# A hybrid diffusion backbone on one core: long-convolution filters 256 channels at a time, interleaved with the gates of layer 0

## The chip, the core and the metric

The kernel runs on one core of one Trainium2 chip. A core has a matrix engine (TensorE, "PE" in the profile, with its weight loads shown as "PEld"), a vector engine (VectorE, "DVE"), an activation engine (ScalarE, "ACT"), a general engine (GpSimd, "POOL"), and a sync engine ("SP") that issues this kernel's DMAs. On-chip data lie in SBUF; matmuls write to PSUM, which has eight banks of 512 fp32 columns. The metric is the time of one execution in device microseconds.

## The reference, cut to what matters

Four trunk layers run over 512 latent and 256 context tokens of width 1024. Layers 0 and 3 are multi-head latent attention, layer 1 is windowed attention, layer 2 is a Hyena long convolution. Two parts of it are touched by the change.

The gate of an attention layer is a projection of the normalised, modulated input `h`; the attention's output is multiplied by its SiLU:

```
cq_x, ckv_x, kr_x, gate_x = jnp.split(hx @ w_in, split_at, axis=-1)
...
y_x = (o_x.reshape(b, n, A_WIDTH) * jax.nn.silu(gate_x)) @ w_out
```

The filters of layer 2 depend on weights alone, so they can be made at any time before layer 2. A small network gives 64 features for each tap; a product with `f_w3` gives the taps, a decay is multiplied on, and layer 2 needs the transform of the taps (2 orders, 2 directions, 1024 channels, once for 512 and once for 256 taps):

```
h = jnp.sin(freq * (z @ f_w1 + f_b1))
h = jnp.sin(freq * (h @ f_w2 + f_b2))
h = (h @ f_w3).astype(jnp.float32).reshape(n, 2, C_ORDER, C_WIDTH)
...
return h * jnp.exp(-t[:, :, None, None] * deltas)
```

## The kernel before, in words

**Numbers.** fp32 values are split in a high part (rounded to a shorter float by ScalarE) and a low part (the rest, by VectorE or GpSimd), and each product is three matmuls: high x high, high x low, low x high.

**Memory.** Two arenas in SBUF are managed by hand: `R` for split operands (118 KB in each partition and a further 24 KB, the "swing") and `F` for fp32 (54 KB). `rl` and `fl` take long-lived blocks from the bottom; `rs` and `fs` take staging slots (8 KB and 4 KB) from the top. `turns_r` and `turns_f` say among how many free slots the one that was freed longest ago is chosen. In PSUM there are four single banks (`a()`, in turn) and two pairs of banks (`s()`, in turn; `halves()` are the four banks of the two pairs).

**Streams of weights.** `W` is the queue of all weights in the order of their use. `take` hands out the next one; `pump` goes ahead: it issues DMAs into fp32 slots (at most `cap_d` staged) and makes high and low parts (at most `cap_w` held). `M` is the same for the modulation weights `w_mod`, which aren't split. A mod unit is 2 MB of `w_mod` in four pieces (`mod_chunk`, L434), 16 matmuls and, for shift and scale, four transposes. The four units of layer 0 must be done before its input can be modulated; later units are "fillers", spread over the layers.

**Order.** The program states an order, and a scheduler that simulates the engines turns it into one fixed order for each engine: an instruction that it expects to be ready may pass an earlier one that it expects to wait. On the chip every engine keeps to its fixed order.

**The start** (`run`, L1668 to L1683) is one loop of steps. `filters` is a generator: before its first `yield` lie the small network, the first `f_w3` weights, the transform table and the decays. Then come 24 steps and 3 for the last spectrum. There are eight groups (c, o, e): 512 channels, order, even or odd part. In `taps` (L1356) each of six tap tiles has two matmuls (L1369), a product with the decay on VectorE (L1371), a high part on ScalarE (L1375) and a low part on GpSimd (one of six on VectorE, L1377). `spectrum` (L1388) of the group before has 30 matmuls (L1397) into PSUM pairs, a ScalarE copy (L1401), two VectorE operations (L1402, L1403), and DMAs to `kd` in DRAM (L1407). The loop puts the four mod units of layer 0 at steps 4, 8, 12 and 16, and the six `pre` (L530: norm, transposes, modulation and split of a token tile of `h`) at every second step from 16 on. At steps 25, 27 and 29 the first weights of layer 0 are pumped.

**Layer 0** (`layer_A`, L691): keys for six tiles (L734, 320 columns), queries for six tiles (L762, 512 columns), six filler units among them; each tile is normalised (`normed`, L701) and transposed. Then come the gates (L769): eight groups of 128 channels, each 48 matmuls (`mm_ch`, L588) into single banks, half of them of 512 columns and half of 256, then `gate2` (L344: tanh on ScalarE, one VectorE operation). Then `rotary`, values, projections, the attention, and `w_out_phase` (L592), in which the next layer's `pre` run. Layer 3 uses the same code for 512 query tokens. In `layer_A` the low parts of weights are made by VectorE (`lo_pool` False); during the start they are made by GpSimd.

Of the kernel before, what the change touches and what calls it, by code (L numbers as in the profile page):

```python
# [19 lines left out]
P = 128  # L20
D = 1024
KD = 8
# [8 lines left out]
WX = {25: (3, 2), 27: (3, 2), 29: (3, 3)}  # L31
# [10 lines left out]
MI = (4, 8, 12, 16)  # L42
PS = 16
PD = 2
WP = 2

R_WORDS = 118 * 256
F_WORDS = 54 * 256 - 64
# [222 lines left out]
class Kern:  # L271
    def __init__(self, ctx, tc, io):
# [16 lines left out]
        self.fillers, self.mg = [], {}  # L289

# [301 lines left out]
    def w_out_phase(self, L, og, wkey, order, last, hook):  # L592
# [11 lines left out]
        for n, t in enumerate(order):  # L604
# [43 lines left out]
        if nxt is not None:  # L648
            self.W.pump(self.W.cap_w + 1, self.W.cap_w)
        for b in g:  # L650
            b.free()
# [20 lines left out]
    def want_A(self, L, j, ctx_out):  # L672
        io = self.io
        w = io["a_w_in"][j].rearrange("(k p) n -> p k n", p=P)
        for k in range(0, KD, 2):
# [3 lines left out]
        for c in range(8):  # L679
            self.W.want(("gate", c), w[:, :, 832 + P * c:960 + P * c])  # L680
# [10 lines left out]
    def layer_A(self, L, j, h, ctx_out, last):  # L691
# [5 lines left out]
        og = self.fl(KD * T)  # L697
# [69 lines left out]

        spans = [(0, NX), (NX, NC)] if ctx_out else [(0, NX)]
        for c in range(8):  # L769
# [480 lines left out]
    def filters(self, j):  # L1250

        nc, io = self.nc, self.io
        self.kd = self.dram.tile([2, 8, P, 1536], F32, name="kd")
        fp = self.fl(4 + 128 + 64)
        fv = fp.ap
        w1, w2 = fv[:, 4:68], fv[:, 68:132]
        zt = self.fl(T)
# [13 lines left out]
        sdr = Ring(self, "rl", 2 * 6 * 512, 2)  # L1271
        w3r = Ring(self, "rs", 2 * 2 * 512, 2)
# [3 lines left out]
        biasr = Ring(self, "fl", 512, 1)  # L1276

        def load_w3(c, o):

            st = self.fs(1024)  # L1280
            sv = st.v(2, 512)
            for d in range(2):
                c0 = d * 2048 + o * 1024 + 512 * c
                for half in range(2):
                    nc.sync.dma_start(out=sv[64 * half:64 * half + 64, d], in_=w3[:, c0:c0 + 512])
            sd = self.fs(1024)
            sdv = sd.v(2, 512)
            nc.gpsimd.tensor_tensor(sdv[:, 0], sv[:, 0], sv[:, 1], op=ALU.add)
            nc.gpsimd.tensor_tensor(sdv[:, 1], sv[:, 0], sv[:, 1], op=ALU.subtract)
            wv = w3r.next().v(2, 2, 512)  # L1290
            nc.scalar.activation(wv[:, 0], sdv, AF.Copy)
            nc.vector.tensor_tensor(wv[:, 1], sdv, wv[:, 0].bitcast(F32), op=ALU.subtract)
            st.free()
            sd.free()
            wvs[c, o] = wv
            biases[c, o] = bias = biasr.next()
            nc.sync.dma_start(out=bias.ap[0:1], in_=io["c_filt_bias"][j, o:o + 1, 512 * c:512 * c + 512])

        def load_ft(i):
            for c0, n in ((0, 1024), (1024, 256)):  # L1300
                st = self.fs(n)
                nc.sync.dma_start(out=st.ap, in_=io["ftab"][:, i, c0:c0 + n])
                nc.scalar.activation(ftv[:, i, 0, c0:c0 + n], st.ap, AF.Copy)
                nc.gpsimd.tensor_tensor(ftv[:, i, 1, c0:c0 + n], st.ap, ftv[:, i, 0, c0:c0 + n].bitcast(F32), op=ALU.subtract)
                st.free()

        two_pi = 2 * math.pi
# [490 lines left out]
```

## Time and profile before

| | us |
|---|---|
| median of 3 runs | 1953.55 (1951.68 to 1954.86) |
| profiled execution | 1953.32 |
| its span in the trace | 1951.5 |
| TensorE busy in the span | 1820.0 (93%) |
| VectorE busy | 1182.5 (61%) |
| first matmul of the filters | 23.4 |
| first key matmul of layer 0 | 150.6 |
| first and last gate matmul of layer 0 | 239.7, 313.2 |

How to read the rows: a group's row has the line, the engine, the operation, the tile written and those read, the shape, the count, then busy time, mean ns of one, and the idle time of the engine just before them with what ended it. In the timeline and in the chain of waits a row starts with its start and duration in us; brackets hold the idle time ahead of it and its releaser. A row of the table of stretches has the stretch, its length, busy time (and instructions) of PE, PEld, DVE, ACT and POOL, the granted clock, the share of time that the DMA engines were busy and GB/s. Matmuls are pipelined, so a matmul's duration is longer than the distance to the next one's start. DMA rows give count, KB each and us from issue to landing.

### The profile page before, as it was taken

To read this page: it belongs to the slowest core of one execution; us is meant where nothing else is said; L and a number is where in the kernel's file an instruction comes from. 1 tells how busy PE (TensorE), PEld (TensorE's weight loads), DVE (VectorE), ACT (ScalarE), POOL (GpSimd) and SP (SyncE) were. 2 spreads that over 40 slices of the span, in tenths; PEclk is the share of its full clock that TensorE was granted. 3 is DMA by queue.
4 is the path that set the end of the run, shared out by engine and by line. 5 is a ranking of instruction groups with operands and counts; after the bars stand their busy time and mean duration, and the time that the engine had idled before them with its cause. 6 is when DMAs were issued, how large, how long until landed. Compare 5 with 4: busy or idle time off the path is not lost.

```text
span 1951.5 us, 30304 instructions
## 1 busy us (share of the span) xinstructions
PE 1820.0 (93%) x11628; PEld 1576.6 (81%) x11628; DVE 1182.5 (61%) x2364; ACT 812.3 (42%) x1686; POOL 521.6 (27%) x523
## 2 busy tenths in 40 slices
PE   5879799999999899999989899999998998999998
PEld 3557588999988888888868699999987777889986
DVE  6684134787755367676675445566668553477663
ACT  3473132555544255565664422222222343354451
POOL 5561000000213321221231344444445221000120
PEclk9999899999999999999999999999999999999999
DMA  7857521001133112222362622222221335310121
GB/s 214 259 175 226 158 78 31 22 24 43 44 109 117 57 48 83 76 67 67 99 223 103 204 60 85 70 74 76 76 77 60 122 120 154 87 33 23 44 76 54
DMA packets 186356, 186.31 MB, mean 95 GB/s; under 512 B 16600, under 2 KB 164952, under 8 KB 186212
## 3 DMA queue, kind: packets, MB, share of 16 engines
q1 hardware_dynamic: 186212, 184.39, 30.6%
q8 instruction: 91, 1.49, 0.3%
q14 instruction: 53, 0.43, 0.1%
HBM read 160.24 MB, written 24.12 MB: 94 GB/s over the span
## 4 chain that ended last, share of the span: by engine, by line
PE 77%; DVE 10%; DMA 6%; ACT 3%; issue 3%; POOL 1%; SPq 0%; POOLq 0%; DVEq 0%; ACTq 0%
PE pb L588 13%; PE pb L622 11%; PE pa L588 10%; PE pb L873 5%; PE pa L912 4%; PE pa L1068 3%; PE pa L1049 3%; DMA arena_f<-in_w_mod_dram 3%; PE pa L1525 2%; PE pa L1558 2%; PE pa L442 2%; PE pa L898 2%; PE pa L1177 2%; PE pb L577 2%; PE pb L578 2%
## 5 line engine op out<-in xcount | busy, mean ns | idle before, releaser
L588 PE MATMUL pb<-arena_r 128*128 128x512 f32 (+1 forms) x1536 | 293.2, 345 | 8.1 <-DVE arena_f L1498 3.6
L588 PEld LDWEIGHTS pb<-arena_r 128*128 128x128 f32 x1536 | 239.3, 192 | 40.7 <-issue 3.8
L341 ACT ACTIVATE arena_r<-pa 128x384 fp32r<-128x384 f32 (+2 forms) x382 | 175.3, 478 | 198.5 <-PE pa L898 68.2
L342 DVE TENSOR_TENSOR arena_r<-pa,arena_r 128x384 fp32r<-128x384 f32 (+2 forms) x382 | 199.7, 537 | 86.6 <-ACT arena_r L341 84.9
L588 PE MATMUL pa<-arena_r,swing_R 128*128 128x512 f32 (+1 forms) x816 | 165.9, 355 | 0.6 <-DVE arena_r L342 0.4
L588 PEld LDWEIGHTS pa<-arena_r,swing_R 128*128 128x128 f32 x816 | 132.2, 188 | 21.8 <-DVE arena_r L342 0.6
L873 PE MATMUL pb<-arena_r 128*128 128x384 f32 (+1 forms) x720 | 141.4, 337 | 3.0 <-ACT arena_r L341 1.8
L233 POOL TENSOR_TENSOR swing_R<-arena_f,swing_R 128x1024 fp32r<-128x1024 f32 (+1 forms) x33 | 77.1, 2340 | 200.5 <-ACT swing_R L230 150.7
L873 PEld LDWEIGHTS pb<-arena_r 128*128 128x128 f32 x720 | 119.0, 188 | 5.1 <-ACT arena_r L341 2.5
L668 POOL TENSOR_TENSOR arena_f<-arena_f 128x128 f32<-128x128 f32 (+1 forms) x44 | 20.9, 474 | 364.1 <-DVE small L881 180.1
L622 PE MATMUL pb<-arena_r 128*128 128x512 f32 x480 | 115.2, 393 | 0.0
L358 POOL TENSOR_SCALAR small<-small 128x1 f32<-128x1 f32 x68 | 17.8, 262 | 349.1 <-ACT trash L564 135.6
L622 PEld LDWEIGHTS pb<-arena_r 128*128 128x128 f32 x480 | 89.5, 188 | 20.0 <-issue 1.1
L233 POOL TENSOR_TENSOR arena_r<-swing_F,arena_r 128x1024 fp32r<-128x1024 f32 x34 | 84.6, 2492 | 76.0 <-ACT arena_r L230 73.9
L912 PE MATMUL pa<-arena_r 128*128 128x256 f32 x624 | 91.4, 286 | 2.1 <-DVE arena_r L342 2.1
L912 PEld LDWEIGHTS pa<-arena_r 128*128 128x128 f32 x624 | 81.7, 190 | 4.8 <-ACT arena_r L341 2.5
L1068 PE MATMUL pa<-swing_R,arena_r 128*128 128x256 f32 x576 | 80.2, 289 | 5.1 <-DVE arena_f L348 3.8
L877 DVE TENSOR_REDUCE small<-pb 128x1 f32<-128x768 f32 (+1 forms) x80 | 67.5, 846 | 21.6 <-PE pb L873 20.7
L880 ACT ACTIVATE arena_f<-pb,small 128x768 f32<-128x768 f32 (+1 forms) x80 | 65.2, 816 | 32.9 <-DVE small L878 26.5
L1068 PEld LDWEIGHTS pa<-swing_R,arena_r 128*128 128x128 f32 x576 | 72.9, 192 | 7.3 <-DVE arena_f L348 5.2
L442 PE MATMUL pa<-arena_f,cst 128*32 128x256 f32 x744 | 57.0, 407 | 23.3 <-DMA arena_f<-in_w_mod_dram 23.0
L230 ACT ACTIVATE arena_r<-swing_F 128x1024 fp32r<-128x1024 f32 x34 | 36.2, 1063 | 101.5 <-PE pb L588 93.7
(266 smaller groups left out, 4239.6 us busy)
## 6 DMA issues: line engine op xcount, KB each, us to landing
arena_f<-in_w_mod_dram SPq DMA_DIRECT2D x93, 512.0 KB, 4.8
swing_F<-in_c_w_in_dram SPq DMA_DIRECT2D x31, 512.0 KB, 4.1
kd<-arena_f SPq DMA_DIRECT2D x48, 256.0 KB, 3.4
arena_f<-in_a_w_in_dram SPq DMA_DIRECT2D x24, 512.0 KB, 4.2
arena_f<-kd SPq DMA_DIRECT2D x16, 768.0 KB, 4.5
arena_f<-in_b_w_in_dram SPq DMA_DIRECT2D x20, 512.0 KB, 4.2
x<-arena_f SPq DMA_DIRECT2D x18, 512.0 KB, 4.1
arena_f<-in_a_w_out_dram SPq DMA_DIRECT2D x16, 512.0 KB
```

The source lines that it names most:

```text
L233: eng.tensor_tensor(lo, view, hi.bitcast(F32), op=ALU.subtract)
L341: self.nc.scalar.activation(hi, src, AF.Copy)
L342: self.nc.vector.tensor_tensor(lo, src, hi.bitcast(F32), op=ALU.subtract)
L442: nc.tensor.matmul(ps[32 * j:32 * j + 32, n0:n0 + 256], self.cst[:, 4 * kh + j, :], w[:, j, :], start=(kh == 0), stop=(kh == 1), skip_grou ...
L588: nc.tensor.matmul(out, l, rhs(part, k, i), start=(k == 0 and q == 0), stop=(k == kt - 1 and q == 2))
L622: nc.tensor.matmul(ys[:, 512 * hf:512 * hf + 512], ov[:, part, k], wt[:, 0, 512 * hf:512 * hf + 512], start=(k == 0 and q == 0), stop=(k = ...
L873: nc.tensor.matmul(S[:, 512 * b:512 * b + w], l, r[:, k0 + w * b:k0 + w * b + w], start=(q == 0), stop=(q == 4))
L877: nc.vector.tensor_reduce(mx, Sv, axis=AX.XY, op=ALU.max)
L880: nc.scalar.activation(pr.v(nb, w), Sv, AF.Exp, bias=mx, scale=sc, accum_out=sm)
L912: nc.tensor.matmul(o[:, 0:256], vv[:, a_, kt % 3, P * hh:P * hh + P], ptv[i // nh][:, b_, i % nh], start=(i == 0 and q == 0), stop=(i == n ...
L1049: nc.tensor.matmul(o, l[:, k], self.h_at(h, part, k, t0, n), start=(k == 0 and i == 0), stop=(k == KD - 1 and i == 2))
L1068: nc.tensor.matmul(ps[:, 0:256], self.h_at(h, part, k, P * t, P), w, start=(k == 0 and i == 0), stop=(k == KD - 1 and i == 2))
```

## The change

- **Width.** `filters` works on 256 channels: 16 groups of 3 steps. A step of `taps` takes two tap tiles, with four matmuls of 256 columns side by side in one bank, and then one decay product, one high part and one low part of 512 columns as before. `spectrum` makes the short transform alone and the two long ones together. Its outputs leave in 96 DMAs of 128 KB in place of 48 of 256 KB. The `f_w3` pieces and decays have half the width; `f_w3` is fetched at the start of a group and split at its end. Weights and decays take less room in `R` and `F`.
- **Start.** The network is cut by `yield`s; mod units 0 and 1 of layer 0 are stated next to its two layers, units 2 and 3 at steps 6 and 12. The six `pre` come at every step from 13 on, each with a `W.pump(2, 1)`.
- **Gates.** For the first layer the gate weights stand first in `W`. From step 19 on, `gates_A` is advanced by two `yield`s (two of the eight k's of a group, 12 matmuls) ahead of each step of the filters. Its products go to the PSUM pairs (in layer 3 too, where the gates keep their place); meanwhile `spectrum` uses single banks (`self.gating`). The block `og` (24 KB of `F`) is taken at step 19, with `turns_f` at 1 from step 17 and at 4 from step 19.
- **Elsewhere.** `turns_r` is 1 when `w_out_phase` of layer 0 pumps the first weights of layer 1. `F` has 16 words more.

```diff
-MI = (4, 8, 12, 16)
-PS = 16
-PD = 2
-WP = 2
+MI = (6, 12)
+PS = 13
+PD = 1
+GS = 19
+GR = 2
...
+                    self.turns_r = 1 if nxt == 1 else 3
...
+    def gates_A(self, ogv, h, spans):
+
+        for c in range(8):
+            blk, (wh, wl) = self.W.take(("gate", c))
+            ps = self.s()
+            outs = [ps[:, t0:t0 + n] for t0, n in spans]
+            for k in range(KD):
+                for q, (l, part) in enumerate(((wh, 0), (wh, 1), (wl, 0))):
+                    for (t0, n), out in zip(spans, outs):
+                        self.nc.tensor.matmul(out, l[:, k], self.h_at(h, part, k, t0, n), start=(k == 0 and q == 0), stop=(k == KD - 1 and q == 2))
+                if k < KD - 1:
+                    yield
+            blk.free()
+            for (t0, n), o in zip(spans, outs):
+                self.gate2(ogv[:, c, t0:t0 + n], o)
+            yield
...
-        for c in range(8):
-            if units and c >= UC:
-                self.fill()
-                units -= 1
-            blk, (wh, wl) = self.W.take(("gate", c))
-            outs = [self.a()[:, 0:n] for _, n in spans]
-            self.mm_ch(outs, lambda part, k, i: self.h_at(h, part, k, *spans[i]), lambda k: (wh[:, k], wl[:, k]))
-            blk.free()
-            for (t0, n), o in zip(spans, outs):
-                self.gate2(ogv[:, c, t0:t0 + n], o)
+        if not gated:
+            for _ in self.gates_A(ogv, h, spans):
+                pass
...
+        CW = 256
...
-        groups = [(c, o, e) for c in range(2) for o in range(2) for e in range(2)]
+        groups = [(c, o, e) for c in range(4) for o in range(2) for e in range(2)]
...
                 ps = self.a()
-                for part in range(2):
-                    nc.tensor.matmul(ps, h2.ap[:, P * lt:P * lt + P], wv[:, part, e], start=(part == 0), stop=(part == 1))
+                for l2 in range(2):
+                    for part in range(2):
+                        nc.tensor.matmul(ps[:, CW * l2:CW * l2 + CW], h2.ap[:, P * (lt + l2):P * (lt + l2) + P], wv[:, part, e],
+                                         start=(part == 0), stop=(part == 1))
...
-            for fi in (2, 0, 1):
-                pab = self.s().rearrange("p (a n) -> p a n", a=2)
+            for fis in ((2,), (0, 1)):
+                n = len(fis)
+                if n == 1:
+                    ps = self.a()
+                    pa = [ps[:, 0:CW], ps[:, CW:2 * CW]]
+                elif self.gating:
+                    pa = [self.a(), self.a()]
+                else:
+                    ps = self.s()
+                    pa = [ps[:, 0:2 * CW], ps[:, 2 * CW:4 * CW]]
...
-        start = iter(pres())
+        next(steps, None)
+        unit(0)
+        next(steps, None)
+        unit(1)
+        next(steps, None)
+        start, gates, og = iter(pres()), iter(()), None
+        done = False
         for i in range(99):
             if i == LS:
                 self.setup_late()
...
+            if i == GS - 2 and early:
+                self.turns_f = 1
+            if i == GS and early:
+                self.turns_f = 4
+                og = self.fl(KD * T)
+                self.gating = True
+                self.W.cap_d, self.W.cap_w = 2, 4
+                gates = self.gates_A(og.v(KD, T), h, [(0, NX), (NX, NC)] if DEPTH > 1 else [(0, NX)])
+            for _ in range(GR):
+                next(gates, None)
+            done = done or next(steps, 1) == 1
+            if done and i > GS:
                 break
```

More of the change, by code (lines that the diff above doesn't have):

```diff
@@ L649, in w_out_phase @@
             self.W.pump(self.W.cap_w + 1, self.W.cap_w)
+        self.turns_r = 3
         for b in g:
@@ L678, in want_A @@
             self.W.want(("cq", k), w[:, k:k + 2, 0:512])
-        for c in range(8):
-            self.W.want(("gate", c), w[:, :, 832 + P * c:960 + P * c])
+        if not gates_first:
+            gates()
         wq = io["a_w_q"][j].rearrange("(k p) (h c) -> p k h c", p=P, h=8)
@@ L1256, in filters @@
         w1, w2 = fv[:, 4:68], fv[:, 68:132]
+        decr = [self.fl(2 * CW) for _ in range(4)]
+        tmps = Ring(self, "fl", 2 * CW, 2)
+        biasr = Ring(self, "fl", CW, 1)
         zt = self.fl(T)
@@ L1305, in load_ft, with load_dec @@
                 st.free()
+        LTS = [4, 0, 2]
+        dec = {}
+        def load_dec(c, n):
+            b, lt = decr[(3 * c + n) % 4], LTS[n]
+            nc.sync.dma_start(out=b.v(2, CW), in_=io["decay"][:, lt:lt + 2, CW * c:CW * c + CW])
+            dec[c, lt] = b
+        w3_0 = fetch_w3(0, 0)
+        ft_0 = fetch_ft(0)
+        for n in range(3):
+            load_dec(0, n)
         two_pi = 2 * math.pi
@@ new lines, in taps @@
+                eng = nc.vector if n == 1 and e else nc.gpsimd
+                eng.tensor_tensor(tvv[:, lt:lt + 2, 1], tmp.v(2, CW), tvv[:, lt:lt + 2, 0].bitcast(F32), op=ALU.subtract)
+                if (o, e) == (1, 1):
+                    if c < 3:
+                        if n < 2:
+                            load_dec(c + 1, n + 1)
+                    else:
+                        if n == 0:
+                            decr[(3 * c + 3) % 4].free()
+                        dec[c, lt].free()
@@ L1631, in run @@
         L = layers[0]
+        early = L % 3 == 0 and 2 in layers
         self.plan_mod(layers)
@@ L1644, in run @@
             if kind == 0:
-                self.want_A(L, j, ctx_out)
+                self.want_A(L, j, ctx_out, early and i == 0)
             elif kind == 1:
@@ L1650, in run, with unit @@
         L = layers[0]
+        def unit(c):
+            for _ in self.mod_ab_unit(L, c):
+                pass
         def pres():
             ts = [0, 1, 2, 3, 4, 5]
-            self.W.cap_d = 2
+            self.W.cap_d, self.W.cap_w = 1, 4
             xts = [self.load_x(L, t) for t in ts[:1]]
@@ L1671, in run @@
                 self.setup_late()
-            if i == MI[3] - 1:
-                self.M.cap_d = self.M.look_d = 0
             if i in MI:
-                for _ in self.mod_ab_unit(L, MI.index(i)):
-                    pass
+                if i == MI[-1]:
+                    self.M.cap_d = self.M.look_d = 0
+                unit(2 + MI.index(i))
             if i >= PS and (i - PS) % PD == 0:
                 next(start, None)
-            if i in WX:
-                self.W.cap_d, self.W.cap_w = WX[i]
-                self.W.pump(*WX[i])
-            if next(steps, 1) == 1 and i > PS + 13:
+            if i == GS - 2 and early:
[10 more added lines that the diff above has]
+            if done and i > GS:
                 break
+        for _ in gates:
+            pass
+        self.gating = False
         self.M.cap_d = self.M.look_d = 1
@@ L1689, in run @@
             if kind == 0:
-                h = self.layer_A(L, j, h, ctx_out, last)
+                h = self.layer_A(L, j, h, ctx_out, last, og if i == 0 else None)
             elif kind == 1:
```

145 lines of the change are left out of this document (69 added, 76 removed).

## The prediction

> **What bounds the kernel now.** I read the busy tenths first, then the busy times of stretches cut at the stage borders, then TensorE's timeline in each stretch. Line numbers are those of the kernel before.
>
> ```profile
> PE   5879799999999899999989899999998998999998
> ```
>
> TensorE (PE) is the bound almost everywhere; only the first 240 us (slices of 48.8 us) have room. The stretches below are: the filters' small network; filters with the last w_mod pieces; filters up to the first `pre`; filters with the six `pre`; keys and queries with six filler units; the gates.
>
> ```profile
> core 0: us, PE busy (x) PEld busy (x) DVE busy (x) ACT busy (x) POOL busy (x), PEclk, DMA share, GB/s
> 0.00:23.40 23.40, 3.12 (x9) 0.65 (x9) 13.87 (x17) 7.25 (x11) 10.89 (x14) 1.00 0.75 232
> 23.40:68.20 44.80, 42.57 (x210) 29.89 (x210) 31.70 (x53) 19.83 (x33) 27.09 (x20) 0.96 0.74 215
> 68.20:108.30 40.10, 31.22 (x164) 20.09 (x165) 24.32 (x41) 17.59 (x29) 22.75 (x19) 0.91 0.80 241
> 108.30:150.60 42.30, 32.15 (x148) 24.64 (x147) 39.68 (x64) 29.57 (x56) 27.45 (x22) 0.96 0.66 185
> 150.60:239.70 89.10, 77.09 (x518) 56.05 (x517) 27.58 (x62) 22.93 (x53) 9.72 (x28) 0.94 0.64 200
> 239.70:313.30 73.60, 73.60 (x421) 64.46 (x420) 22.89 (x35) 20.45 (x39) 2.67 (x6) 1.00 0.22 58
> ```
>
> TensorE idles 20.3, 2.2, 8.9, 10.2, 12.0 and 0.0 us. The `pre` stretch is VectorE's (39.68 of 42.30). The gates have TensorE full while DVE and the DMAs lie idle: they are the filler, the filters the place with holes. The change brings the two together. The holes before the `pre` are waits for w_mod, as is the largest one among the queries:
>
> ```profile
> 71.59 1.93 PE L442 MATMUL pa<-arena_f,cst 128*32 128x256 f32 x16 [3.42 <-DMA arena_f<-in_w_mod_dram]
> 91.51 1.49 PE L442 MATMUL pa<-arena_f,cst 128*32 128x256 f32 x16 [3.59 <-DMA arena_f<-in_w_mod_dram]
> 208.98 3.64 PE L442 MATMUL pa<-arena_f,cst 128*32 128x256 f32 x32 [6.83 <-DMA arena_f<-in_w_mod_dram]
> ```
>
> **The work that must be done before the keys.** Before, the keys start at 150.6 and the gates come later. Moved ahead of the keys they take what the chain of waits gives them:
>
> ```profile
> 239.75 5.45 PE pa L588 x24
> 251.61 6.84 PE pa L588 x41
> 258.89 54.28 PE pa L588 x317
> ```
>
> That is 66.6 us, so the old order, with the gates put ahead, would reach the keys at 150.6 + 66.6 = 217.2. That is the number to beat.
>
> Halving the filters' width turns 336 matmuls of 512 columns into 672 of 256. Prices by start to start:
>
> ```profile
> 37.76 3.07 PE L1397 MATMUL pb<-swing_R,arena_r 128*128 128x512 f32 x12
> 40.67 0.63 PE L1369 MATMUL pa<-arena_r 128*128 128x512 f32 x2
> ...
> 618.26 0.28 PE L577 MATMUL pb<-swing_R,arena_r 128*128 128x256 f32 x1
> 619.91 0.27 PE L579 MATMUL pb<-swing_R,arena_r 128*128 128x256 f32 x1
> ```
>
> Twelve of 512 took 2.91 (0.243 each), fourteen of 256 took 1.65 (0.118). So 336 x 0.243 = 81.6 against 672 x 0.118 = 79.3: -2. The gates' 382 matmuls, half of either width, took 0.174 each, which leaves 2 x 0.174 - 0.118 = 0.231 for one of 512: 77.6, so +2. I take 80 both times, the edit at nothing.
>
> The other terms of the filter stretch, in groups:
>
> ```profile
> L1371 DVE TENSOR_TENSOR arena_f<-pa,arena_f 128x512 f32<-128x512 f32 x48 | 31.8, 681 | 22.1 <-PE pa L1369 15.2 <-POOL arena_r L1377 3.9 <-POOL swing_R L1377 3.0
> L1402 DVE TENSOR_TENSOR arena_f<-arena_f,pb 128x512 f32<-128x512 f32 x23 | 15.6, 676 | 2.1 <-ACT arena_f L1401 2.1
> L1401 ACT ACTIVATE arena_f<-pb 128x512 f32<-128x512 f32 x23 | 13.7, 595 | 12.7 <-PE pb L1397 9.8 <-DMA kd<-arena_f 2.9
> L442 PE MATMUL pa<-arena_f,cst 128*32 128x256 f32 x128 | 10.7, 447 | 7.1 <-DMA arena_f<-in_w_mod_dram 7.0
> L556 DVE TENSOR_TENSOR arena_r<-arena_f,arena_r 128x1024 fp32r<-128x1024 f32 x5 | 7.6, 1518 | 1.0 <-ACT arena_r L555 1.0
> L550 DVE TENSOR_SCALAR arena_f<-pa,ab 128x128 f32<-128x128 f32 x20 | 6.8, 394 | 0.0
> L543 PE MATMUL pa<-ident,arena_f 128*128 128x128 f32 x40 | 5.4, 278 | 5.6 <-DVE arena_f L537 5.6
> L537 DVE TENSOR_SCALAR arena_f<-arena_f,small 128x1024 f32<-128x1024 f32 x5 | 5.2, 1046 | 0.3 <-DMA kd<-arena_f 0.3
> L459 PE MATMUL pa<-ident,arena_f 128*128 128x128 f32 x16 | 2.4, 272 | 0.0
> ```
>
> TensorE: a mod unit (10.7 + 2.4)/4 = 3.3; six tiles' transposes 5.4 x 48/40 = 6.5; the network 3.1. Sum with gates: 3.1 + 80 + 13.2 + 6.5 + 66.6 = 169.4 us, against 217.2 elapsed: 47.8 us are idle or run at half clock. VectorE: one `pre` 1.05 + 1.52 + 4 x 0.39 = 4.1, six 24.8. The filters' VectorE time is the three stretches' 95.7 less the 19.6 of L556, L550 and L537 in them, 76 in all, 1.6 for each of the 48 new steps. The new widths leave its elements as they were (48 products of 512 as now); ScalarE and POOL likewise, so these edits go at nothing.
>
> **The new order, stage by stage.** (1) Mod units 0 and 1 stand beside the network and fill 6.6 of its 20.3 idle us. (2) The `pre` need all four units. Ahead of the last w_mod piece lie 16 pieces of 0.52 MB, 2.4 of tables and constants, 1.0 of w3, 1.0 of decay, about 2.6 of kd and 0.5 of x: 16 MB by the shapes in the code. At the 215 to 241 GB/s of the first three stretches that is 66 to 74 us; VectorE's pace alone (thirteen steps of 1.6 at the 0.71 share of the second stretch) would allow 53. I take 68. Meanwhile filters can run ahead: 44.6 x 0.71 / 1.6 = 20 steps. (3) Six `pre` at the 0.94 share of the old `pre` stretch: 26 us, to 94. The 512-column halves of the first gate need only tiles 0 to 3 and slip in: 24 x 0.231 = 5.5. By then TensorE has done 3.1 + 13.2 + 33 + 6.5 + 5.5 = 61. (4) Left are 108 us with no starved engine: VectorE has 28 steps x 1.6 = 45 plus the gates' own few. At a share of 0.97 that takes 111: 205, **12 us early**.
>
> The other end: TensorE works in a fixed order, so a late piece holds what is queued behind it, filters included (the two waits of 3.4 and 3.6 above). If filters stand at step 13 when the pieces land at 70, the six `pre` and six steps of filters cost (24.8 + 9.6)/0.94 = 37, to 107, and 109/0.97 more gives 219: 2 us late. And with data not limiting, 15 us early. I take **-8**, nearer the first, since those two waits hold only 7 of 85 us.
>
> (5) Keys and queries. The six fillers (12.6 MB) set the pace; their pieces are issued from first to last row:
>
> ```profile
> 155.86 4.50 SPq L211 DMA_DIRECT2D arena_f<-in_w_mod_dram  x3
> ...
> 225.04 6.25 SPq L211 DMA_DIRECT2D arena_f<-in_w_mod_dram  x2
> ```
>
> 75 us for 24 pieces. Gate weights no longer pass through this queue, and key and query weights can be fetched while the gates run at 58 GB/s. Of 12.0 idle us between nothing and 10 go. The gates no longer fill holes here (24 matmuls at 239.75 did), and pieces still come two at a time. I take **-4**. What is late next: the rotary products follow the queries at once, and their weights must be split in this stage: 0 to +4, I take **+1**.
>
> (6) In layer 3 the gates now use the wide PSUM pair, whose first half the last query tile holds until it is normalised:
>
> ```profile
> 221.87 0.70 ACT trash L704 x2
> 222.92 0.56 POOL small L359
> 223.50 0.76 DVE arena_f L707
> ```
>
> 221.87 to 224.26, up to 2.4 us; a gate on the other pair may cover it. **+1.5**.
>
> (7) `turns_r` of 1 puts layer 1's first split weights into the top slots. Before, the second is copied at 608.60, some ten us ahead of the key matmuls quoted above (618.26):
>
> ```profile
> 608.60 1.07 ACT L230 ACTIVATE swing_R<-arena_f 128x1024 fp32r<-128x1024 f32 x1
> ```
>
> A slot still read by that last tile costs up to +3; a fresher one gains nothing, since with that margin the keys wait for something else. **0**.
>
> Sum -8 - 4 + 1 + 1.5 = -9.5. The profiled execution took 1953.3 (span 1951.5), beside a median of 1953.55. Forecast **1944 us**.
>
> **A rule against it.** Gate weights' low halves move from DVE to POOL:
>
> ```profile
> L233 POOL TENSOR_TENSOR swing_R<-arena_f,swing_R 128x1024 fp32r<-128x1024 f32 (+1 forms) x33 | 77.1, 2340 | 200.5 <-ACT swing_R L230 150.7
> 7.24 0.36 DVE L1324 TENSOR_SCALAR arena_f<-arena_f 128x384 f32<-128x384 f32 x1
> 13.32 7.43 POOL L1304 TENSOR_TENSOR arena_r<-arena_f,arena_r 128x1024 fp32r<-128x1024 f32 x4
> 13.46 2.45 DVE L1324 TENSOR_SCALAR arena_f<-arena_f 128x384 f32<-128x384 f32 x1
> ```
>
> The same DVE instruction took 0.36 us alone and 2.45 beside POOL. Eight splits of 2.34 are 18.7 us of POOL, in a stage with VectorE half idle. The Trainium skill's page "SBUF — State Buffer", section "Who interferes with whom", says that such pairs exclude one another for a whole instruction, whichever came first. By that rule up to 18.7 us of DVE time would be lost and the sum would stand as it is, since only the first gate's split (2.3 us) falls among the `pre`: at worst 1946.
>
> **Rivals.** *Better (B)*: data do not limit, and ten of the twelve idle us of the queries go: -15 - 10 + 2.5 = -22.5, **1931**. For it: DMA share was only 0.75 early. Against: the 16 MB.
>
> *No gain (C)*: the change only moves the holes; the late w_mod pieces hold the filters (the +2 above): +2 - 4 + 2.5, **1954**. For it: three waits for w_mod in the trace. Against: all pieces of two units are now asked for at once.
>
> *Slower (D)*: once the 24 KB for the gates are taken, four 4 KB slots are left for staging: two gate weights, the next w3 piece in half of the groups, and the spectrum's output. That output holds its slot through 0.60 on ScalarE, 2 x 0.68 on DVE, two to four issues of 0.36 and the landing:
>
> ```profile
> 152.23 0.36 SPq L1407 DMA_DIRECT2D kd<-arena_f  x1
> ...
> kd<-arena_f SPq DMA_DIRECT2D x48, 256.0 KB, 3.4
> arena_f<-in_a_w_q_dram SPq DMA_DIRECT2D x48, 128.0 KB, 2.6
> ```
>
> 0.60 + 1.36 + 0.72 + 2.6 = 5.3 to 0.60 + 1.36 + 1.44 + 3.4 = 6.8 us. A group has two outputs and lasts 111/9.7 = 11.5 us, so with one slot free it decides once an output takes over 5.75 us, and outweighs the gain when each of ten groups loses 1 us (6.2). The next output's ScalarE copy then waits, and ScalarE's queue behind it: taps, gate tanh, weight splits, then TensorE. At 6.8 in all ten groups: 2 x 6.8 - 11.5 = 2.1 each, 21 in all; with half of the groups at two slots 11. I take 17 on top of -9.5: **1961**. For it: L1401 already waited 2.9 us for a kd write, with more slots. Against: TensorE can run gates meanwhile. The page "DMA: Bandwidth & Descriptors" of the Trainium skill, section "Bandwidth", asks to batch to at least 1 MiB; by it 96 writes of 128 KB in place of 48 speak for D too.
>
> **Chances.** Forecast (1938 to 1949) 0.42, B 0.16, C 0.21, D 0.21. A change under 0.2% (3.9 us) cannot be told here: faster 0.58 (forecast and B), same 0.21 (C), slower 0.21 (D). The range 1929 to 1961 takes in most of B and D.
>
> **What would show it.** Right: keys begin at 205 to 213; TensorE is full from about 95 on; w_mod pieces of unit 3 land near 68; the queries' hole of 6.8 shrinks. C: gates begin after 105 behind w_mod waits. D: L1401's successor waits on kd writes, with TensorE idle inside the gates. Wrong in another place: more than 3 us new idle after the queries, or in layers 1 and 3.

## The result, and the profile after

The changed kernel is **slower**: 1967.99 us (median of 5 runs, 1964.23 to 1969.23) against 1951.68 us for the kernel before in the same job (1945.62 to 1954.86), a ratio of 1.0082 with an interval of 1.0059 to 1.0104. The forecast was 1944, the range ended at 1961.

The first view is the busy time of stretches of the changed kernel, with the prediction's columns. The borders are its own: the network with two mod units; filters up to unit 3; the six `pre`; the gates among the filters; keys, queries and rotary up to layer 0's first scores.

```profile
core 0: us, PE busy (x) PEld busy (x) DVE busy (x) ACT busy (x) POOL busy (x), PEclk, DMA share, GB/s
0.00:20.10 20.10, 5.12 (x25) 1.06 (x25) 9.71 (x17) 5.47 (x9) 5.76 (x12) 1.00 0.77 230
20.10:71.00 50.90, 38.70 (x298) 28.85 (x299) 25.37 (x46) 17.21 (x31) 22.18 (x19) 0.92 0.80 249
71.00:111.60 40.60, 29.38 (x161) 26.21 (x159) 38.16 (x63) 31.03 (x60) 29.59 (x25) 0.73 0.58 165
111.60:225.60 114.00, 113.96 (x776) 105.34 (x777) 62.08 (x102) 41.07 (x73) 46.80 (x35) 1.00 0.46 126
225.60:343.00 117.40, 104.21 (x714) 82.86 (x712) 43.72 (x103) 33.76 (x83) 14.85 (x40) 0.97 0.49 147
```

The gates do what was hoped of them: 113.96 of 114.00 us full. But they start late. The `pre` stretch takes 40.6 us with VectorE busy for 38.16 of them, TensorE for 29.38 at a granted clock of 0.73. TensorE's timeline shows why it begins at 71: it stands for unit 3.

```profile
63.52 1.60 PE L1441 MATMUL pb<-arena_r 128*128 128x256 f32 x12
67.66 0.64 PE L443 MATMUL pa<-arena_f,cst 128*32 128x256 f32 x8 [2.55 <-DMA arena_f<-in_w_mod_dram]
70.63 1.12 PE L460 MATMUL pa<-ident,arena_f 128*128 128x128 f32 x4 [2.33 <-ACT arena_f L456]
...
111.64 2.70 PE L710 MATMUL pb<-arena_r,swing_R 128*128 128x256 f32 x14 [1.98 <-DVE arena_r L557]
```

The same places in the traces, in us from the start of the span, with a second profiled execution of the changed kernel and the narrow filters alone (both below):

| place on TensorE | before | after | after, again | narrow filters alone |
|---|---|---|---|---|
| keys begin | 150.6 (217.2 with the gates) | 225.6 | 227.3 | 165.0 |
| layer 0's first scores | 340.9 | 343.0 | 345.1 | 358.4 |
| end of layer 0's output product | 616.5 | 622.8 | 624.6 | 633.2 |
| end of layer 1's | 1085.0 | 1094.9 | 1094.2 | 1099.2 |
| end of layer 2's | 1594.5 | 1606.0 | 1604.7 | 1612.0 |
| last product | 1943.3 | 1959.0 | 1957.5 | 1960.4 |

So layer 0 loses 6.3 us (8.1 in the second execution), layers 1 and 2 together 5.2 (2.1), layer 3 4.2 (4.0). Of layer 0's 6.3 us, 2.1 (4.2) are there at its first scores. The other 4.2 (3.9) come between them and the end of the output product, where TensorE is busy for 275.38 us in place of 272.31 and idle 1.1 us longer; no run tells why.

Among the first keys stands a wait of TensorE that the kernel before doesn't have, 3.9 us long in the second execution:

```profile
232.87 0.47 PE L578 MATMUL pb<-swing_R,arena_r 128*128 128x320 f32 x1 [3.61 <-DVE arena_f L349]
```

The second key tile's products wait until the last gate's tanh on ScalarE (L348) and product on VectorE (L349) are done, which read that gate out of its PSUM pair; the keys use the banks of the two pairs. That tanh begins at 229.80, behind weight splits that had themselves waited 3.26 us for their weights.

Adding up each matmul record and the clock granted to it splits TensorE's time up to the last product in three: idle 123.2 before and 120.8 after; lost to half clock 24.8 and 37.9; the rest 1795.2 and 1800.4. The change did remove idle time, 9.1 us in the first 260 us. It came back as half clock, as matmul time, and as idle time at other places.

### The profile page after: what moved, and what is told of

Its sections match the earlier page's. It is cut to its first block, busy times and chain, and to the rows that moved or that the text cites. A ratio compares the mean times of both kernels' runs of the same rounds, so it can differ in the third digit from the quotient of the medians.

```text
span 1967.5 us, 31161 instructions
## 1 busy us (share of the span) xinstructions
PE 1838.3 (93%) x11964; PEld 1608.9 (82%) x11964; DVE 1190.3 (60%) x2386; ACT 815.0 (41%) x1698; POOL 536.4 (27%) x537
## 5 line engine op out<-in xcount | busy, mean ns | idle before, releaser
L233 POOL TENSOR_TENSOR swing_R<-arena_f,swing_R 128x1024 fp32r<-128x1024 f32 (+1 forms) x39 | 92.1, 2368 | 142.8 <-ACT swing_R L230 138.2
L710 PE MATMUL pb<-arena_r,swing_R 128*128 128x512 f32 (+1 forms) x432 | 90.3, 362 | 3.8 <-DVE arena_r L557 2.0
L710 PEld LDWEIGHTS pb<-arena_r,swing_R 128*128 128x128 f32 x432 | 71.7, 190 | 16.3 <-DVE arena_r L557 2.3
```

What stands on the lines that cost most here:

```text
L233: eng.tensor_tensor(lo, view, hi.bitcast(F32), op=ALU.subtract)
L710: self.nc.tensor.matmul(out, l[:, k], self.h_at(h, part, k, t0, n), start=(k == 0 and q == 0), stop=(k == KD - 1 and q == 2))
```

## The experiments

Ratios are to the kernel before, in the same job; its medians there were 1948.3 to 1950.6 us.

### Layer 3's gates: single banks or a pair

Single banks put back in layer 3 of the changed kernel, and pairs put into both gated layers of the kernel before:

```diff
 # changed kernel, layer 3 only
-            for _ in self.gates_A(ogv, h, spans):
-                pass
+            for c in range(8):
+                ...
+                outs = [self.a()[:, 0:n] for _, n in spans]
 # kernel before
-            outs = [self.a()[:, 0:n] for _, n in spans]
+            pg = self.s()
+            outs = [pg[:, t0:t0 + n] for t0, n in spans]
```

> The changed kernel, but the gates of layer 3 go to single PSUM banks as before (layer 0 as changed). Theory 'PSUM pair': TensorE's idle 1.8 us at the first gate of layer 3 and the half-clock window behind it go; keys to first scores of layer 3 fall from 131 to about 128 us, the time by 2 to 4 us, to 1964-1966. Rival 'clock by chance': layer 3 stays at 131 or varies without the wait, time 1968.

> The kernel before, with the gates of layers 0 and 3 on the PSUM pairs (nothing else changed). Theory 'PSUM pair': a wait of about 2 us at the first gate of each layer, time 1954 to 1956 where the kernel before has 1952. Rival: the scheduler covers it with a gate on the other pair, no difference.

Measured: 1961.98 us, **1.0052** (1.0029 to 1.0074), and 1958.99 us, **1.0046** (1.0030 to 1.0062). From the end of layer 2 to the last product, single banks take 348.8 us (before), 347.4 (the first of these runs) and 348.5 (with a second mending, below); pairs take 353.0 and 352.8 (the changed kernel twice) and 353.5 (the kernel before with pairs). The means are 4.9 us apart. Over all twenty profiled executions the two groups don't meet: 347.4 to 349.7 in the twelve with single banks, 351.0 to 353.5 in the eight with pairs, 4.1 apart in the mean. **That is what the pair costs layer 3: 4 to 5 us.** The kernel before with pairs is 9.2 us slower in the median than without them, about twice that, and more than either expectation had; its profiled execution (1953.72) is among its fastest and doesn't show the other half. The timelines of ScalarE and TensorE in the changed kernel show the place:

```profile
1675.05 0.60 ACT L732 ACTIVATE trash<-pb 128x512 bf16<-128x512 f32 x1 [4.93 <-issue]
1675.64 1.05 ACT L230 ACTIVATE swing_R<-arena_f 128x1024 fp32r<-128x1024 f32 x1
...
1676.74 1.07 PE L710 MATMUL pb<-arena_r,swing_R 128*128 128x512 f32 x2 [1.77 <-ACT swing_R L230]
```

The second gate's weights are split only behind the last query tile's square, and TensorE waits 1.77 us. The kernel before with pairs has the same wait, to the hundredth, in TensorE's timeline:

```profile
1661.50 0.73 PE L588 MATMUL pb<-arena_r,swing_R 128*128 128x512 f32 x2 [1.77 <-ACT swing_R L230]
```

The wait is only part of the price. Three stretches of 3.41 us of the changed kernel, cut where the clock changes:

```profile
1673.40:1676.81 3.41, 1.64 (x8) 1.01 (x6) 0.13 (x1) 1.63 (x3) 0.74 (x2) 1.00 0.00 0
1676.81:1680.23 3.42, 3.42 (x11) 2.63 (x12) 2.45 (x3) 0.60 (x1) 0.00 (x0) 0.52 0.11 11
1680.23:1683.64 3.41, 3.41 (x16) 2.78 (x15) 0.00 (x0) 0.60 (x1) 0.00 (x0) 0.98 1.17 263
```

A cell that TensorE filled for 1.64 of 3.41 us is followed by one at half clock, worth another 1.7 us.

### The gates: where they stand, and what the interleaving is worth

The gates stated behind all filter steps but still ahead of the keys; and back behind the queries, with the narrow filters and the new start kept:

```diff
 # first: nothing in the loop, all gates after it
-            for _ in range(GR):
-                next(gates, None)
 # second
-        early = L % 3 == 0 and 2 in layers
+        early = False
...
+            if i in WX:
+                self.W.cap_d, self.W.cap_w = WX[i]
+                self.W.pump(*WX[i])
```

> The changed kernel, but the gates' products are stated behind all steps of the filters (still ahead of the keys): the interleaving alone is undone. Theory 'the start is late, but the interleaving works': filters without gates run at VectorE's pace (28 steps x 1.6 us at a share of 0.8 from 112 us on, to 168), then 66.6 us of gates: keys at about 234, 9 us later than with the change, time 1977. Rival 'interleaving is worth nothing, slots and banks hold the filters anyway': keys at 225, time 1968.

> The changed kernel with layer 0's gates back behind its queries, and nothing interleaved: narrow filters, the new start (units 0 and 1 beside the network, 2 and 3 ahead of steps 6 and 12, `pre` from 13), key weights fetched at the filters' last steps as before, the split arena laid out as before. Theory (the interleaving earns what the narrow filters cost): slower than the changed kernel by 6 to 14 us, 1973 to 1981, with layer 0's scores at 349 to 357. Rival (the new start alone earns it): 1965 to 1969.

Measured: **1.0103** (1.0071 to 1.0136) and **1.0177** (1.0160 to 1.0195). With the gates behind the queries the kernel is 18 us slower than the changed one, and layer 0's scores come at 362.0 in place of 343.0 (expected were 349 to 357). So standing ahead of the keys and alternating with the filters are together worth more than the prediction gave them. Gates behind the filters reach the keys 15.9 us later (241.5; the theory had 234) and end only 2.4 us later in the profiled executions; the two intervals overlap, so how much of the gain is in the alternation and how much in standing ahead of the keys is not settled.

### The narrow filters alone

The kernel before with the changed `filters` and nothing else: steps, mod units, `pre` and fetches at the same shares, gates after the queries.

```diff
-MI = (4, 8, 12, 16)
-PS = 16
-PD = 2
+MI = (8, 16, 24, 32)
+PS = 32
+PD = 4
 def filters(self, j):
+    CW = 256
     ...
```

> The kernel before with the changed filters alone: 256 channels at a time, 48 steps in place of 24, mod units, `pre` and fetches at the same share of the filters, the split arena laid out as before; gates after the queries as before. Theory (the narrower filters cost TensorE time of their own: 672 matmuls at 0.120 us against 336 at 0.231 are +3, and their groups' busy time grew from 97.2 to 105.4 us): keys 3 to 8 us later, end +3 to +8, 1953 to 1958. Rival (the width costs nothing, as the prediction took it): 1950 +- 2.

Measured: 1970.10 us, **1.0100** (1.0079 to 1.0121). The edit that the prediction put at nothing costs, alone, about as much as the whole change (the intervals overlap), and more than either expectation had. It is the whole of the new `filters`: `f_w3` fetches, decays, tap buffers and PSUM banks are regrouped with the width, and apart from the tap buffers none of these was tried alone. The stretches of this kernel: network, filters up to the last unit, `pre`, and from the keys to the scores:

```profile
0.00:21.70 21.70, 3.09 (x8) 0.61 (x8) 11.64 (x16) 6.83 (x11) 8.29 (x14) 1.00 0.72 221
21.70:116.10 94.40, 78.95 (x605) 66.97 (x605) 64.04 (x110) 36.36 (x65) 48.48 (x43) 0.96 0.73 216
116.10:165.00 48.90, 36.74 (x256) 33.32 (x252) 40.25 (x71) 32.02 (x63) 26.01 (x24) 0.93 0.54 153
165.00:358.40 193.40, 176.98 (x1115) 147.18 (x1116) 69.97 (x141) 55.82 (x119) 18.04 (x43) 0.96 0.40 119
```

Before, the last unit was done at 101.7 us, here at 116.1; the `pre` stretch is as long as before (48.9), and 3.1 us more go until the scores. No engine is full in the slow stretch: TensorE 78.95 of 94.40, VectorE 64.04. TensorE's busy time hides the loss, since a matmul counts as busy until it has drained (0.28 us for 256 columns that follow each other every 0.120). So I counted stops: a matmul that starts over 0.06 us later than the width of the one ahead of it asks for. From the first tap to the last unit the kernel before has 50 stops, 16.1 us in all; the narrow one 101, 27.5 us, 89 of them under 0.45 us. That is 11.4 us; the matmuls themselves, at 0.120 for 256 columns against 0.231 for 512, account for another 3 over the whole stage.

Two things go beside this count. At the same share of the steps, the narrow kernel has more spectrum products behind it, since its spectra trail the taps by a group that is half as large: up to the last unit the trace has 465 tap and spectrum products of 256 columns, against 215 of 512 before. That is 35 more of 256, 4.2 us at 0.120. And the stops have several owners. Mod units, which wait for pieces of w_mod, hold about 8 of the 16.1 us before and 11 of the 27.5; tap and spectrum products hold about 8 and 17. Over all of the filters, TensorE's idle time in front of spectrum products until a tap is split (high part on ScalarE, low part on GpSimd) grows from 1.5 to 8.7 us.

### What causes the stops

Some suspects were taken away, doubled or moved. The first are VectorE's small operations: the bias row is now added sixteen times in place of eight, at a price that hardly falls with the width. By groups, up to the last unit, first the narrow kernel, then the kernel before:

```profile
L1385 DVE SCALAR_TENSOR_TENSOR arena_f<-arena_f 1x256 f32<-1x256 f32 x12 | 7.5, 638 | 0.1
```

```profile
L1373 DVE SCALAR_TENSOR_TENSOR arena_f<-arena_f 1x512 f32<-1x512 f32 x6 | 4.1, 679 | 0.1
```

```diff
 # narrow kernel without the bias
-                if e == 0 and lt in (0, 4):
-                    nc.vector.scalar_tensor_tensor(tmp.ap[0:1, 0:CW], bias.ap[0:1], ...)
 # narrow kernel with three tap buffers
-        tmps = Ring(self, "fl", 2 * CW, 2)
+        tmps = Ring(self, "fl", 2 * CW, 3)
```

> The kernel before with the narrow filters (1970.1), and the bias of the filters' first row left out: sixteen VectorE operations on one row of 256, 0.64 us each, that the wide filters had eight times at 0.68. What is left out is the bias term alone. Theory (the narrow filters are slow since operations that don't shrink with their width are doubled on the chain from VectorE over ScalarE to GpSimd): 10 us less VectorE work in the filters, end -5 to -9. Rival (VectorE has room there, 15 of 20 us busy): 0 to -2.

> The kernel before with the narrow filters (1970.1), and three buffers between VectorE's product and the split of a tap in place of two, as the wide filters had. Theory (a chain with two buffers stalls VectorE until GpSimd's 1.32 us split is done): end -4 to -10, keys from 165 to 155 to 161. Rival (VectorE waited only 4.3 us for GpSimd's splits, and what is slow lies elsewhere): 0 to -3.

Measured: **1.0114** (1.0096 to 1.0133) and **1.0133** (1.0115 to 1.0152). Without the bias the last unit comes at 109.1, 7 us earlier, but the scores at 356.9, 1.5 earlier: a gain that the later stretches eat. The third buffer gains nothing (keys at 167.1, where the theory had 155 to 161).

The next suspect is SyncE's queue: twice as many writes, 0.50 us of issuing each, ahead of the w_mod pieces.

```diff
 # kernel before: 96 writes of 128 KB in place of 48 of 256
+                    for u in (0, 2):
...
 # narrow kernel, kernel before, mended changed kernel: issued by ScalarE
-                        nc.sync.dma_start(out=dst, in_=kov...
+                        nc.scalar.dma_start(out=dst, in_=kov...
```

> The kernel before, each write of the filters' spectra to kd split in two (96 of 128 KB in place of 48 of 256 KB), nothing else. Theory (the narrow filters are late since SyncE issues 0.50 us for each of twice as many writes, and the w_mod pieces queue behind them): 24 us more issuing until the keys, keys from 150.6 to 157 to 166, end +5 to +15. Rival (issues have room beside the filters, the price is on VectorE, ScalarE and GpSimd): 0 to +3.

> The kernel before with the narrow filters (1.0100 of before), their 96 writes to kd issued by ScalarE in place of SyncE. Theory (SyncE's queue): keys from 165 to 152 to 160, end -5 to -15. Rival (ScalarE then waits for VectorE's sums ahead of each write, and its taps behind it; or the queue was no limit): -3 to +5.

> The kernel before, its 48 writes to kd issued by ScalarE in place of SyncE. Theory (SyncE's queue holds w_mod already before the change: 3.42 and 3.59 us of waits): -2 to -6. Rival (nothing gained, ScalarE waits instead): -1 to +4.

Measured: **1.0002** (0.9991 to 1.0013), **1.0177** (1.0161 to 1.0193), **1.0006** (0.9993 to 1.0020). Doubling the writes costs the kernel before nothing, and ScalarE as their issuer makes the narrow kernel 15 us worse. This theory fell.

The last suspect is the latency of a tap: it takes VectorE, ScalarE and GpSimd in turn (0.68, 0.63 and 1.32 us), whatever the width of its group, and a group is now half as long.

```diff
-            prev = spectrum(*g)
+            pend.append(g)
+            prev = spectrum(*pend.pop(0)) if len(pend) == 2 else iter(())
-        sdr = Ring(self, "rl", 2 * 6 * 512, 2)
+        sdr = Ring(self, "rl", 2 * 6 * CW, 4)
```

> The kernel before with the narrow filters (1.0100), the spectra two groups behind the taps in place of one (four buffers of half a group's width: the same room). Theory (a tap takes 0.68 on VectorE, 0.63 on ScalarE and 1.32 us on GpSimd whatever the width of the group, so a group half as long leaves its spectrum half the time until the taps are ready; TensorE stops between groups): last unit from 116 to 102 to 110, keys from 165 to 153 to 160, end -5 to -12. Rival (the loss is in the pieces' own start and end on TensorE, or in fetches): -3 to +3.

Measured: 1979.39 us, **1.0142** (1.0120 to 1.0165): slower still. The last unit does come at 101.5, as in the wide kernel (101.7), and the stops up to it fall from 101 to 58 (16.8 us, wide: 16.1). What follows gives it back; the stretches up to the last unit, the `pre`, and from the keys to the scores:

```profile
21.70:101.50 79.80, 70.12 (x555) 62.04 (x555) 58.39 (x101) 31.61 (x58) 42.38 (x37) 0.91 0.75 221
101.50:161.70 60.20, 45.53 (x303) 42.34 (x304) 50.10 (x86) 37.89 (x73) 33.22 (x31) 0.86 0.60 176
161.70:353.70 192.00, 175.78 (x1116) 146.22 (x1115) 67.19 (x135) 54.15 (x116) 16.16 (x42) 0.96 0.40 119
```

VectorE had done 5.7 us less when the last unit landed (58.39 against 64.04) and makes it up among the `pre`, 60.2 us in place of 48.9. At the scores 4.7 of the 17.5 us are left of the gain, and between the scores and the end of layer 1 this kernel loses 17.0 us against the narrow one, with the same code there. Why, I don't know; its TensorE work is the same, with 8.8 us more idle and 3.5 more lost to half clock up to the start of layer 1's output product.

Does the early last unit show that the taps' latency was the cause? TensorE's waits up to the last unit say no. First the narrow kernel, then this one:

```profile
PE pa L443 <- DMA arena_f<-in_w_mod_dram: 9.3, 6, 4.0
PE pb L1420 <- POOL swing_R L1389: 1.8, 2, 1.4
PE pa L1420 <- ACT swing_R L1387: 0.6, 1, 0.6
```

```profile
PE pa L443 <- DMA arena_f<-in_w_mod_dram: 0.8, 1, 0.8
PE pb L1420 <- ACT arena_r L1387: 3.4, 2, 2.9
PE pb L1420 <- POOL arena_r L1389: 1.2, 1, 1.2
PE pb L1420 <- POOL swing_R L1389: 1.0, 1, 1.0
```

(A row has what TensorE waited for, the sum in us, the number of waits and the longest.) What went are the waits for w_mod, 8.5 us, and 50 products that now stand behind the unit, 6.0 us at 0.120; the unit is 14.6 us earlier. The waits of spectra for split taps, which the theory was about, grew, and over all of the filters they are 13.8 us in place of 8.7. The distance wasn't kept either: at 56.31 TensorE stands at the fifth group's spectrum with 16 steps, five groups and a third, of tap products done, since the scheduler may let a spectrum pass taps.

So the waits between the engines are longer in the narrow kernel, and none of these edits makes it faster. What makes the waits longer is open.

### The start: units, splits, and mending

```diff
 # all four units ahead of the steps
-MI = (6, 12)
-PS = 13
-GS = 19
+MI = ()
+PS = 1
+GS = 7
...
-                    self.W.pump(2, 1)
+                    self.W.pump(1, 1)
...
+        unit(2)
+        self.M.cap_d = self.M.look_d = 0
+        unit(3)
 # units later
-MI = (6, 12)
-PS = 13
-GS = 19
+MI = (9, 19)
+PS = 20
+GS = 26
 # splits on VectorE until the gates start
+            self.lo_pool = False
...
+                self.lo_pool = True
```

> The changed kernel with all four mod units stated ahead of the first step of the filters, the six pre at steps 1 to 7 and the gates from step 7 (only one gate weight fetched ahead of them). Theory 'the gates start late because the last pieces of w_mod are asked for behind kd writes and other loads': pieces land by 45-50 us, the pre end near 88, keys at 205 to 215, time 1948 to 1957. Rival 'the pre are slow by themselves, since GpSimd and VectorE hold one another up': the pre take 40 us here too, and keys come no earlier than 220, time 1962 or more.

> The changed kernel with mod units 2 and 3 ahead of filter steps 9 and 19 in place of 6 and 12, the `pre` from step 20 and the gates from step 26. Theory (in program order TensorE stands at step 13 behind unit 3's late piece; with more filter steps ahead of it that wait is filled): TensorE idle between 20 and 112 us falls from 29.5 by 5 to 10, keys at 216 to 221, end -4 to -8. Rival (the pieces are issued late since SP waits for the filters' copies, so that more steps ahead of them make them later still): the last piece lands after 80 us, keys at 223 to 230, end -2 to +4.

> The changed kernel with the low halves of the gate weights that are split during the six `pre` taken on VectorE in place of GpSimd. Theory (GpSimd's 2.3 to 3.3 us splits hold VectorE off, so that L557 takes 2.4 us and the `pre` stretch 40 us in place of 26): that stretch 4 to 8 us shorter, keys at 218 to 222, end -3 to -6. Rival (VectorE is full there anyhow and only gets four splits more): keys at 225 or later, end 0 to +4.

Measured: units first **1.0216** (1.0186 to 1.0245), later **1.0170** (1.0150 to 1.0191). Units first does bring the keys to 213.4, but filters run on until 237.1 beside them and the scores come at 352.9, ten us later than in the changed kernel. Later units go the rival's way and further: the last one is done at 89.0, the keys begin at 243.1 (the rival had 223 to 230). The schedule chosen is better than both.

Splits on VectorE: 1959.85 us, **1.0049** (1.0031 to 1.0067). The edit moved one split of the four that run beside the `pre`: VectorE makes the first at 79.17, but the other three are still on GpSimd, at 84.34, 97.42 and 109.14, since `lo_pool` is True again by the time the program states them. The groups of the `pre` stretch, first of the changed kernel, then of this one:

```profile
L557 DVE TENSOR_TENSOR arena_r<-arena_f,arena_r 128x1024 fp32r<-128x1024 f32 x6 | 11.1, 1867 | 0.0
```

```profile
L557 DVE TENSOR_TENSOR arena_r<-arena_f,arena_r 128x1024 fp32r<-128x1024 f32 x6 | 7.8, 1314 | 0.0
```

VectorE's instruction is 0.55 us shorter in the mean. In the changed kernel it takes 1.20 and 1.21 us where GpSimd was idle as it began, and 1.65 to 2.59 us the four times that a GpSimd instruction was under way; a tap's split that GpSimd began 0.06 us behind it (at 105.63) took 2.32 us, where others took 1.28. That is the contention which the Trainium skill's page "SBUF — State Buffer" states in its section "Who interferes with whom" for a VectorE instruction with two inputs in SBUF beside a GpSimd instruction that reads SBUF; the trace agrees. But although the six take 3.3 us less here, the keys still begin at 225.6 and the scores at 343.9: the theory's way to the gain is not what happened. The profiled gain lies in layers 1 and 2 (976.1 us against 983.2 and 980.1 of the two executions of the changed kernel), where the code is the same. That part stays unexplained.

> The changed kernel once more, with nothing altered, beside the experiments on its start. Theory (part of the +16 is where the half-clock windows fall): a second profiled execution shows the keys at 225 +- 2 us and layer 3's scores about 5 us later against their layer's start than before, but other half-clock windows, at the end of layer 1 above all, where the first execution lost 6.8 us at half clock; ratio 1.004 to 1.010. Rival (the end of layer 1 is late because of the change, through another order of prefetches): the same 5 us are lost there again.

The changed kernel again: 1967.28 us, **1.0082** (1.0061 to 1.0103). Keys at 227.3; from 960 to 1100 us it lost 3.1 us to half clock in place of 6.5, and layer 1 is then 1.1 us longer than before in place of 3.6: part of that loss was chance.

> The changed kernel with two mendings at once: layer 3's gates on single banks (alone 1.0052), and the gate weights' low halves that fall among the `pre` on VectorE (alone 1.0049). Theory (two separate places, so the two gains of about 6 and 7 us add up): 1952 to 1957, ratio 1.001 to 1.003. Rival (both gained by where the half-clock windows fell, and the gains overlap): 1958 to 1962.

> The changed kernel with both mendings (1.0048 together) and its 96 writes to kd issued by ScalarE. Theory (SyncE's queue delays the last w_mod piece, issued at 61.8 us, and x tile 3, for which the `pre` wait until 86 us): pieces 5 to 10 us earlier, keys 218 to 222, end -4 to -8 against 1.0048. Rival (ScalarE's waits for VectorE take its place): -2 to +4.

> The changed kernel with both mendings (1.0048 together) and the spectra two groups behind the taps (three buffers). Theory (the same stops between groups hold its first nineteen steps, and with them the mod units and the `pre`): TensorE's idle time between 20 and 112 us falls by 4 to 8, keys at 218 to 223, end -3 to -8, ratio 1.000 to 1.003. Rival (its start waits for w_mod pieces and for VectorE among the `pre`, not for taps): -2 to +3.

Both mendings together: 1958.04 us, **1.0048** (1.0033 to 1.0064), no better than either, though in its profile layer 3 has 4.5 us back (348.5 against 353.0). With ScalarE's writes **1.0066** (1.0050 to 1.0083), with the longer lag **1.0076** (1.0060 to 1.0092); their keys begin at 231.5 and 233.8, later than the 226.2 without them, where the theories had 218 to 223. No version of the change beat the kernel before.

## Why the prediction was wrong

**The width, an edit at nothing.** This is the step that failed: "336 x 0.243 = 81.6 against 672 x 0.118 = 79.3: -2", "+2", and then "the new widths leave its elements as they were ... so these edits go at nothing". The matmul price was nearly right (+3). But alone, the new `filters` cost 20 us (1.0100), 16.7 of them by the end of layer 0. Work counted in elements left out the waits between the engines: up to the last unit the narrow kernel has 11.4 us more of stops, and over all of the filters 7.2 us more of waiting for split taps. That the step was wrong is shown by the run; why the waits are longer is open.

**Term by term,** the trace splits the +15.7 us up to the last product so. Stages (1) to (4), forecast -8, came out at +8.4 (keys at 225.6 against 217.2). Stage (5), forecast -4 and +1, came out at -6.3. Layer 3, forecast +1.5, came out at +4.2. Two parts had no term, or one of 0: from layer 0's first scores to its end +4.2, layers 1 and 2 +5.2.

**Stages (2) and (4), -8.** The prediction let filters run ahead to step 20 while the pieces landed at 68. The pieces did land there: unit 3 begins at 67.66. But unit 3 stands ahead of step 12 in TensorE's order, and ahead of it TensorE had done thirteen steps and no more. I had this as the other end ("filters stand at step 13", gates from 107, keys at 219) and set it aside because two waits held "only 7 of 85 us"; the program's order decides it, not the share of waits. The rest up to 225.6 is stage (3): 26 us for six `pre` alone, 37 with six steps, in fact 40.6 with nine (13 to 22), and 114 us for what followed instead of 112. Of the tests named, "TensorE is full from about 95" and "keys begin at 205 to 213" failed; "w_mod pieces of unit 3 land near 68" and "the queries' hole of 6.8 shrinks" (the longest wait for w_mod there is now 1.9) came true. Gates from 111.6 on, with a wait for w_mod ahead of the `pre`, is near to what rival C named, at 1954. Nor did the prediction's rule against itself count right: not "only the first gate's split" fell among the `pre` but four, of 2.4 to 3.3 us on GpSimd, three of which the program states later. What they cost the stretch is not settled: the one run on it moved a single split, and its keys came no earlier.

**(5), -4 and +1.** Right in sign, half the size: from the keys to the scores 117.4 us, where the old order had 190.3 - 66.6 = 123.7, so -6.3, and that with the new wait of 3.6 us in it, on the pair that (6) priced for layer 3 alone.

**Layer 0 in sum.** Forecast -8 - 4 + 1 = -11; it came out at +6.3. The narrow filters alone gave +16.7 there, which leaves -10.4 for all the rest. That this is near the forecast -11 is bookkeeping, not proof, since the stops that the width makes alone are partly filled once gates stand between them: from 111.6 to 225.6 there is one stop, of 0.1 us.

**(6), +1.5.** Right place, wrong size and wrong owner: 4 to 5 us. Not the tile's hold on the pair but the weight split behind its square, 1.77, and the half-clock cell that it brings.

**(7), 0.** Not run alone. From the end of layer 0 to layer 1's first scores the changed kernel took 69.4 us (692.2 - 622.8), the kernel before 70.7, so nothing speaks against it there. In the kernel with later units TensorE waited 3.6 and 1.6 us at layer 1's start for just such splits.

**Clock.** No step priced it. The change lost 13.1 us more to half clock while losing 2.4 us less to idling. By the same sum, 7.1 of the 13.1 lie in the `pre` stretch (8.8 against 1.7), where VectorE is the fuller engine; so the 13.1 need not all be time lost.

**Rivals.** D did not happen: TensorE has no idle time inside the gates. The Trainium skill's page "DMA: Bandwidth & Descriptors", section "Bandwidth", asks for large transfers, and the prediction let that speak for D; twice as many writes of half the size cost 1.0002, so no run here shows it.

**Layers 1 and 2**, +5.2 and +2.1 in two executions, are open. Their sum lies between 974 and 985 us in all the kernels run, changed or not, but two: 997.4 with units first and 992.0 with the lag in the narrow kernel.

## What to carry to other kernels

An edit that leaves the number of elements as it was is not thereby free: here a new width cost 20 us in waits that no sum of busy times held. Run such an edit alone before anything is built on it. Where an experiment moves the place that you measure at, count the work ahead of that place in both kernels, and read which waits went, before you take it for proof. Read where a late operand stands in the order of TensorE's program before letting other work run ahead of it. And try a gain apart from what it is tied to: here the gates ahead of the keys and among the filters earned 18 us, but they came with an edit that cost 20 alone.

## What was not expected of the hardware

The granted clock changes on a fixed grid of 3.413 us, with another phase in each execution. Over the twenty profiled executions, a cell at full clock in which TensorE was busy for 10 to 50% of the time was followed by one at half clock in 259 of 347 cases; at 50 to 60% in 20 of 151, at 60 to 70% in 3 of 288, above 70% in none of 10,143. Nearly empty cells don't fit a plain rule: below 10% it was 28 of 73. So one wait of about 1.7 us can cost as much again, if it falls into one cell, since a cell at half clock is worth 1.7 us; half of it in each of two cells would leave both over 70% busy, and by these counts cost nothing more. The Trainium skill's page "TensorE: Matmul & The Clock Gate", section "What's actually happening", gives the same free-running window of 3413 ns and the half clock, but lets the clock drop after an idle window; here a half-empty one was enough.
